# A feed-forward's second matrix product: the plain blocked form against seven block products

## The chip, the core and the metric

One core of a Trainium2 chip. The metric is device time of one execution in microseconds (us), median of the runs. TensorE (PE) multiplies, VectorE (DVE) and ScalarE (ACT) do element-wise work, SyncE (SP) issues nearly all DMA transfers, GpSimd (POOL) has almost nothing to do here. All data are fp32. A difference of under 0.2% is not told from none.

## What is computed

One layer of a hybrid decoder, on 1024 tokens of width 1024. Four mixers come first; the change touches only what follows them:

```python
xn = rmsnorm(h, norm_ffn_w)
gate_up = xn @ w_ffn_in                       # 1024 x 5632
g_ff, u_ff = jnp.split(gate_up, [D_FF], axis=-1)   # D_FF = 2816
h = h + (jax.nn.silu(g_ff) * u_ff) @ w_ffn_out     # 2816 x 1024
return rmsnorm(h, norm_f_w)
```

The last two lines are the *second matrix*: activations (1024 x 2816) times `w_ffn_out` (2816 x 1024), the residual `h` added, and a norm over each row.

## The kernel before

**Precision by three products.** A fp32 operand is split into a high part (an ACT cast to fp32r) and a low part (a DVE subtraction). Each block product is three matmuls: high by high, high by low, low by high. A matmul here takes 128x128 of one operand and 128x512 of the other.

**First matrix.** `ffn_in(j)` makes block j of 22 (128 columns of D_FF, all 1024 tokens): seven block products of 12 matmuls, 84 in all, from operand sums that are already on the chip, with additions from the accumulator banks into SBUF, SiLU on ACT and a multiplication on DVE (lines 1142 to 1144). `prepare(j + 1)` loads and splits the next block's weights (lines 1025 to 1050) in between: its gate half and its up half are two loads on SP. Line 1145 stores a block's result, 128 x 1024, to a DRAM tile `asp[j]`. `j` even uses the four banks `pd`, `j` odd the banks `pq` and `pt`.

**Second matrix.** Two halves of the tokens (`hf`), and in each the 22 blocks j, four tiles of 128 tokens, two halves of the columns, three matmuls (lines 1201 to 1203 in `tile_block`). `load_block(n)` loads a block's weights (line 1156, 512 KB), splits them (1158, 1159), loads the block's activations from `asp` (1166, 256 KB) and splits these (1167, 1168). The last three blocks of a half (`LATE`) are run tile by tile, so that one tile of tokens after the other is finished: line 1224 adds the residual, 1225 squares, `rstd_of` (lines 212 to 222) makes the row's factor by small operations and a square root on ACT, 1230 scales, and 1231 stores the output from ACT's queue.

**Order.** The engines run their own instructions in order. A tile framework has put them in each engine's list in an order of its own, and added the waits. SBUF tiles come from `slot` (128x1024), `half` (128x512) and a ring `tmp` of four 128x512 buffers, `t` in the rows.

Of the kernel before, what the change touches and what calls it, by code (L numbers as in the profile page):

```python
# [38 lines left out]
P = 128  # L39
T = 1024  # L40
D = 1024
# [4 lines left out]
NFF = DFF // P  # L46
EPS = 1e-6
H = 512
# [23 lines left out]
def trunk(ctx: ExitStack, tc: tile.TileContext, x, w_in, w_branch, w_out, w_fin, w_fout, prm_d, gw_d, lw_d,  # L72
          nfw_d, snw_d, cst_d, msk_d, out):
    nc = tc.nc
    V, A, G, TE = nc.vector, nc.scalar, nc.gpsimd, nc.tensor
    mult, add, sub, mx, mn = ALU.mult, ALU.add, ALU.subtract, ALU.max, ALU.min

    cp = ctx.enter_context(tc.tile_pool(name="cp", bufs=1))
    sm = ctx.enter_context(tc.tile_pool(name="sm", bufs=3))
# [21 lines left out]
    slot = Slots("s", 26, (P, T))  # L101
    half = Slots("x", 32, (P, H))
    tmp = ring("t", 4, (P, H))
    wraw = ring("wr", 2, (P, T))
    whi = ring("wh", 2, (P, T), dt=F32R)
    wlo = ring("wl", 2, (P, T), dt=F32R)
    dense_bank = ring("pd", 4, (P, H), pp)
    sbank = ring("pq", 2, (P, H), pp)
    tbank = ring("pt", 2, (P, H), pp)
    bank_at = [0]  # L110

    def allbank():
# [54 lines left out]
    for t in range(NT):  # L167
# [5 lines left out]
        if t % 4 == 3:  # L173
            c = C_LX + t // 4 * P
# [8 lines left out]
    def hs(hf):  # L183
        return slice(hf * H, (hf + 1) * H)
# [23 lines left out]
    def rstd_of(ss, n, inv, table=False):  # L208


        v, r, q = (sm.tile([P, 8], F32, name=a, tag=a)[:, :n] for a in ("v", "r", "q"))
        V.tensor_scalar(v, ss, inv, EPS, op0=mult, op1=add)
        if table:
            A.activation(r, v, AF.Sqrt)
            V.reciprocal(r, r)
        else:
            V.tensor_scalar(r.bitcast(I32), v.bitcast(I32), 1, None, op0=ALU.arith_shift_right)
            V.tensor_scalar(r.bitcast(I32), r.bitcast(I32), -1, 0x5F375A86, op0=mult, op1=add)
        for _ in range(1 if table else 3):
# [235 lines left out]
    for i in range(4):  # L455
        j = A.activation(th[i], th[i], AF.Sqrt, bias=tiny)
# [198 lines left out]
    for i in range(2):  # L655
        w = wv
# [5 lines left out]
    for h in range(4):  # L662
        if h == 3:
# [7 lines left out]
            for t in range(NT):  # L671
                p = dense_bank()
# [29 lines left out]
    for hf in range(2):  # L702
        p = tbank()
# [76 lines left out]
    p = tbank()  # L780
# [22 lines left out]
    for i in range(4):  # L803
        u = sconv(i)
# [144 lines left out]
    dp = ctx.enter_context(tc.tile_pool(name="dp", bufs=1, space=bass.MemoryType.DRAM))  # L949
    hsp = [dp.tile([P, D], F32, name=f"hsp{t}") for t in range(NT)]  # L950
    asp = [dp.tile([P, T], F32, name=f"asp{j}") for j in range(NFF)]

    def two(dt=F32):
        t = slot(dt)
        return t[:, 0:H], t[:, H:T], t
# [139 lines left out]
            slot.free(*wo[0][1])  # L1095


    def ffn_in(j, early=False):
# [12 lines left out]
        y = slot()  # L1111
        u, v, uv = two()
        c21 = tmp()

        def upper():
            product(pa, "A12", "B21", False)
            A.activation(y[:, 0:H], pa, AF.Silu)

        product(pa, "A11", "B11")
        A.copy(u, pa)  # L1120
        yield
        if early:
            upper()
            yield
        product(pd, "S1", "T1")
        yield
        product(pb, "S2", "T2")
        V.tensor_add(u, u, pb)
        yield
        product(pc, "S3", "T3")  # L1130
        V.tensor_add(v, u, pc)
        V.tensor_add(v, v, pd)
        yield
        if not early:
            upper()
# [10 lines left out]
        slot.free(y, uv, *pair.held)  # L1146

    loaded = {}

    def load_block(n):  # L1150

        if n in loaded or n >= 2 * NFF:
            return
        hf, j = n // NFF, n % NFF
        w = wraw()
        nc.sync.dma_start(w, w_fout[j * P:(j + 1) * P, :])
        wh, wl = slot(F32R), slot(F32R)
        A.copy(wh, w)  # L1158
        V.tensor_sub(wl, w, f32(wh))  # L1159
        if n < 2:  # L1160
            h, l, t = two(F32R)
            a = tmp()
        else:
            h, l = half(F32R), half(F32R)
            a = half()
        nc.sync.dma_start(a, asp[j][:, hs(hf)])
        A.copy(h, a)
        V.tensor_sub(l, a, f32(h))
        if n >= 2:
            half.free(a)  # L1170
        loaded[n] = (h, l, wh, wl) if n >= 2 else (h, l, wh, wl, t)

    def drop_block(n):
        b = loaded.pop(n)
        slot.free(*b[2:])
        if n >= 2:
            half.free(b[0], b[1])

    for steps in zip_longest(ffn_in(0, True), ffn_in(1, True)):
# [12 lines left out]
    nfw = slot()  # L1192
    nc.sync.dma_start(nfw, nfw_d.broadcast_to([P, D]))
    LATE = 3

    def tile_block(hf, t, j):
        h, l, wh, wl = loaded[hf * NFF + j][0:4]
        tt = slice(t * P, (t + 1) * P)
        for nh in range(2):
            p = banks[t][nh]  # L1200
            TE.matmul(p, lhsT=h[:, tt], rhs=wh[:, hs(nh)], start=j == 0, stop=False)  # L1201
            TE.matmul(p, lhsT=h[:, tt], rhs=wl[:, hs(nh)], start=False, stop=False)  # L1202
            TE.matmul(p, lhsT=l[:, tt], rhs=wh[:, hs(nh)], start=False, stop=j == NFF - 1)  # L1203

    load_block(1)
    for hf in range(2):
        banks = [[allbank() for nh in range(2)] for t in range(4)]
        for j in range(NFF - LATE):
            load_block(hf * NFF + j + 2)
            for t in range(4):  # L1210
                tile_block(hf, t, j)
            drop_block(hf * NFF + j)
        res = [slot() for t in range(4)]
        for t in range(4):
            nc.sync.dma_start(res[t], hsp[hf * 4 + t])
        for n in range(hf * NFF + NFF - LATE + 2, hf * NFF + NFF + 3):
            load_block(n)
        for t in range(4):
            for j in range(NFF - LATE, NFF):
                tile_block(hf, t, j)  # L1220
            y, sq = slot(), slot()
            ss = sm.tile([P, 8], F32, name="ss", tag="ss")
            for nh in range(2):
                V.tensor_add(res[t][:, hs(nh)], res[t][:, hs(nh)], banks[t][nh])
                A.activation(sq[:, hs(nh)], res[t][:, hs(nh)], AF.Square, accum_out=ss[:, nh:nh + 1])
            V.tensor_add(ss[:, 2:3], ss[:, 0:1], ss[:, 1:2])
            r = rstd_of(ss[:, 2:3], 1, 1.0 / D, True)
            tt = slice((hf * 4 + t) * P, (hf * 4 + t + 1) * P)
            for nh in range(2):
                V.scalar_tensor_tensor(y[:, hs(nh)], res[t][:, hs(nh)], r, nfw[:, hs(nh)], op0=mult, op1=mult)  # L1230
                nc.scalar.dma_start(out[tt, hs(nh)], y[:, hs(nh)])
            slot.free(y, sq)
        for j in range(NFF - LATE, NFF):
            drop_block(hf * NFF + j)
        slot.free(*res)


# ---- launch: one core
# [64 lines left out]
```

## Time and profile before

| | |
|---|---|
| median of 3 runs | 2051.46 us (2050.77 to 2053.79) |
| profiled execution | 2052.34 us |
| its span | 2050.4 us |
| instructions in the span | 23991 |
| PE busy | 2006.1 us (98%), 9892 matmuls |
| DVE busy, ACT busy | 1030.5 us (50%), 632.9 us (31%) |
| mean granted clock of PE | 0.997 |
| chain that ended last | PE 89%, DVE 7%, ACT 2%, issue 1%, DMA 1% |

The span is what the profile sees, from the first instruction to the last; the execution's own time is 1.9 us longer. Busy is the time in which an engine works on an instruction; the chain follows back from the last instruction, at each step, to what released it. A PE that is busy all the time and has the largest share of the chain is the limit over the span as a whole; which wait ends last in a stretch is read from that stretch.

### The profile page before, as it was taken

To read this page: it belongs to the slowest core of one execution; us is meant where nothing else is said; L and a number is where in the kernel's file an instruction comes from. 1 tells how busy PE (TensorE), PEld (TensorE's weight loads), DVE (VectorE), ACT (ScalarE), POOL (GpSimd) and SP (SyncE) were. 2 spreads that over 40 slices of the span, in tenths; PEclk is the share of its full clock that TensorE was granted. 3 is DMA by queue.
4 is the path that set the end of the run, shared out by engine and by line. 5 is a ranking of instruction groups with operands and counts; after the bars stand their busy time and mean duration, and the time that the engine had idled before them with its cause. 6 is when DMAs were issued, how large, how long until landed. Compare 5 with 4: busy or idle time off the path is not lost.

```text
span 2050.4 us, 23991 instructions
## 1 busy us (share of the span) xinstructions
PE 2006.1 (98%) x9892; PEld 1663.1 (81%) x9892; DVE 1030.5 (50%) x1728; ACT 632.9 (31%) x942; POOL 14.2 (1%) x20
## 2 busy tenths in 40 slices
PE   7989999999999999999999999999999999999998
PEld 6779888889888878877779888877888888888886
DVE  6560114765242377566562517268665565554532
ACT  5742112332341111442122323154222232243421
POOL 0000000000000000000000000000000000000000
PEclk9999999999999999999999999999999999999999
DMA  5120111111112110111112014122222222466451
GB/s 172 31 72 11 51 52 32 29 46 42 32 32 61 41 32 21 42 42 31 31 43 66 21 52 154 52 93 83 91 64 93 93 64 91 128 205 221 154 165 41
DMA packets 157772, 147.56 MB, mean 72 GB/s; under 512 B 7472, under 2 KB 134880, under 8 KB 157664
## 3 DMA queue, kind: packets, MB, share of 16 engines
q1 hardware_dynamic: 153824, 136.82, 21.9%
q10 hardware_dynamic: 3840, 9.23, 1.2%
q8 instruction: 77, 1.26, 0.3%
q14 instruction: 31, 0.25, 0.0%
HBM read 126.10 MB, written 19.92 MB: 71 GB/s over the span
## 4 chain that ended last, share of the span: by engine, by line
PE 89%; DVE 7%; ACT 2%; issue 1%; DMA 1%; SPq 0%; DVEq 0%; ACTq 0%
PE pd L199 13%; PE pd L200 13%; PE pd L202 13%; PE pd L1106 3%; PE pd L1105 3%; PE pd L1108 3%; PE pd L318 3%; PE pd L316 3%; PE pd L317 3%; PE pd L1202 2%; PE pd L1203 2%; PE pd L1201 2%; PE pq L1108 2%; PE pq L1106 2%; PE pq L1105 2%; PE pt L1105 1%
## 5 line engine op out<-in xcount | busy, mean ns | idle before, releaser
L199 PE MATMUL pd<-x,wh 128*128 128x512 f32 x1056 | 420.1, 398 | 7.4 <-ACT s L348 7.0
L200 PE MATMUL pd<-x,wh 128*128 128x512 f32 x1056 | 418.1, 396 | 0.0
L152 DVE TENSOR_TENSOR wl<-wr,wh 128x1024 fp32r<-128x1024 f32 x82 | 100.4, 1224 | 370.8 <-PE pd L202 264.4
L202 PE MATMUL pd<-x,wl 128*128 128x512 f32 x1056 | 271.9, 394 | 0.0
L199 PEld LDWEIGHTS pd<-x,wh 128*128 128x128 f32 x1056 | 199.4, 189 | 51.8 <-ACT s L348 7.8
L200 PEld LDWEIGHTS pd<-x,wh 128*128 128x128 f32 x1056 | 199.4, 189 | 41.1 <-issue 2.4
L202 PEld LDWEIGHTS pd<-x,wl 128*128 128x128 f32 x1056 | 196.4, 188 | 42.8 <-issue 3.5
L151 ACT CAST wh<-wr 128x1024 fp32r<-128x1024 f32 x82 | 86.3, 1052 | 249.5 <-PE pd L200 227.8
L316 PE MATMUL pd<-s,x 128*128 128x256 f32 (+2 forms) x512 | 159.5, 312 | 0.6 <-ACT s L151 0.6
L318 PE MATMUL pd<-s,x 128*128 128x256 f32 (+2 forms) x512 | 159.8, 312 | 0.0
L317 PE MATMUL pd<-s,x 128*128 128x256 f32 (+2 forms) x512 | 159.6, 312 | 0.0
L370 ACT ACTIVATE s<-pd 128x512 f32<-128x512 f32 x64 | 38.3, 598 | 217.7 <-PE pd L202 217.7
L316 PEld LDWEIGHTS pd<-s,x 128*128 128x128 f32 x512 | 97.4, 190 | 5.7 <-ACT s L151 0.8
L317 PEld LDWEIGHTS pd<-s,x 128*128 128x128 f32 x512 | 97.5, 190 | 5.1
L318 PEld LDWEIGHTS pd<-s,x 128*128 128x128 f32 x512 | 97.5, 190 | 4.8
L199 PE MATMUL pd<-s,wh 128*128 128x512 f32 x256 | 99.8, 390 | 0.0
L200 PE MATMUL pd<-s,wh 128*128 128x512 f32 x256 | 99.8, 390 | 0.0
L382 DVE SCALAR_TENSOR_TENSOR s<-s,pd 128x512 f32<-128x512 f32 x64 | 43.9, 687 | 94.5 <-PE pd L202 94.5
L1159 DVE TENSOR_TENSOR s<-wr,s 128x1024 fp32r<-128x1024 f32 x44 | 53.9, 1225 | 69.0 <-ACT s L1158 54.2
L523 DVE COPY_PREDICATED s<-msk,pq 128x256 f32<-128x256 uint8 x128 | 61.9, 555 | 29.6 <-PE pq L517 16.2
L1025 ACT CAST wh<-wr 128x1024 fp32r<-128x1024 f32 x22 | 23.2, 1055 | 161.7 <-PE pq L1106 79.6
L202 PE MATMUL pd<-s,wl 128*128 128x512 f32 x256 | 68.5, 389 | 0.0
(341 smaller groups left out, 3560.4 us busy)
## 6 DMA issues: line engine op xcount, KB each, us to landing
wr<-in_w_in SPq DMA_DIRECT2D x76, 512.0 KB, 3.6
wr<-in_w_fin SPq DMA_DIRECT2D x44, 512.0 KB, 4.6
wr<-in_w_fout SPq DMA_DIRECT2D x44, 512.0 KB, 3.6
asp<-s SPq DMA_DIRECT2D x22, 512.0 KB, 4.9
x<-asp SPq DMA_DIRECT2D x42, 256.0 KB, 3.9
wr<-in_w_branch SPq DMA_DIRECT2D x16, 512.0 KB, 3.3
s<-in_x SPq DMA_DIRECT2D x8, 512.0 KB, 7.4
wr<-in_w_out SPq DMA_DIRECT2D x8, 512.0 KB, 3.9
```

What stands on the lines that cost most here:

```text
L151: i = A.copy(h, raw)
L152: V.tensor_sub(l, raw, f32(h))
L199: TE.matmul(p, lhsT=wh[k], rhs=ah, start=k == 0, stop=False)
L200: TE.matmul(p, lhsT=wh[k], rhs=al, start=False, stop=False)
L202: TE.matmul(p, lhsT=wl[k], rhs=ah, start=False, stop=k == n - 1)
L316: TE.matmul(p, lhsT=ah, rhs=wh, start=k == 0, stop=False)
L317: TE.matmul(p, lhsT=ah, rhs=wl, start=False, stop=False)
L318: TE.matmul(p, lhsT=al, rhs=wh, start=False, stop=k == n - 1)
L523: V.copy_predicated(dst[:, :, :, side, :], m, pv_[ab][:, i].rearrange("p c (n h) -> p c n h", h=h))
L1105: TE.matmul(p, lhsT=ah[:, k], rhs=bh, start=first and k == 0, stop=False, skip_group_check=True)
L1106: TE.matmul(p, lhsT=ah[:, k], rhs=bl, start=False, stop=False, skip_group_check=True)
L1108: TE.matmul(p, lhsT=al[:, k], rhs=bh, start=False, stop=k == KH - 1, skip_group_check=True)
```

## The change

The second matrix is computed by seven block products (Winograd's form of Strassen's method). The activations are cut into 2 x 2 quarters by tokens (first and second 512) and by even and odd blocks of D_FF; the weights by even and odd blocks and by column halves. Each product has 11 steps (one per pair of blocks), and a step is four tiles of 128 tokens by three matmuls. The products are taken in the order 1, 5, 6, 2, 7, 3, 4 of `steps`.

- **Left sums.** `row_sums(k)`, at the end of each odd `ffn_in`, makes four sums or differences of the pair's activation quarters (lines 1106, 1107, 1108 and, in the next block, 1113) and stores each, 256 KB, to a DRAM tile `ssp[k][i]` (lines 1110, 1114) on SP.
- **Right sums.** `split_step` makes the sums of the weights in place, one DVE subtraction in each step of products 5, 6, 7 and 4 (line 1214).
- **Loads.** `load_step` loads a quarter block of weights, 256 KB, in each step of products 1, 5, 6 and 2 (line 1186) and a quarter block of activations or sums in every step (line 1203), into the `tmp` ring. Loads stand seven steps ahead and splits (1224, 1225) four.
- **ffn_in.** Two intermediate tiles come from the `tmp` ring; the last block takes its product of A12 and B21 early, and steps 0 to 2 are loaded during that block.
- **Ends.** `after(n, t)` adds a product's banks into the result tiles (1291 to 1311); `finish` (1279 to 1285) norms and stores a row tile. Rows 0 to 3 are finished after product 3, at the start of product 4, rows 4 to 7 at the end.

```diff
+    def row_sums(k):
+        y0, y1 = ys_of.pop(2 * k), ys_of.pop(2 * k + 1)
+        a11, a21, a12, a22 = y0[:, 0:H], y0[:, H:T], y1[:, 0:H], y1[:, H:T]
+        s1 = tmp()
+        V.tensor_add(s1, a21, a22)
+        V.tensor_sub(a21, a11, a21)
+        V.tensor_sub(a11, s1, a11)
+        for i, t in enumerate((s1, a11, a21)):
+            nc.sync.dma_start(ssp[k][i], t)
+        def last():
+            V.tensor_sub(a12, a12, a11)
+            nc.sync.dma_start(ssp[k][3], a12)
+            slot.free(y0, y1)
+        later.append(last)
...
-        u, v, uv = two()
+        if own:
+            u, v, uv = two()
+        else:
+            u, v = tmp(), tmp()
...
         A.copy(u, pa)
+        while later:
+            later.pop()()
...
         nc.sync.dma_start(asp[j], y)
+        if j % 2:
+            row_sums(j // 2)
...
+    steps = [(n, k) for n in (1, 5, 6, 2, 7, 3, 4) for k in range(KO)]
+    def load_step(i):
+        n, k = steps[i]
+        if n == 1:
+            we[k] = slot()
+            load_rows(2 * k, 0, we[k])
+        elif n == 5:
+            load_rows(2 * k, 1, we[k])
+        elif n == 6:
+            wd[k] = slot()
+            load_rows(2 * k + 1, 1, wd[k])
+        elif n == 2:
+            load_rows(2 * k + 1, 0, wd[k])
+        a = araw[i] = tmp()
+        nc.sync.dma_start(a, {1: asp[2 * k][:, 0:H], 2: asp[2 * k + 1][:, 0:H], 3: ssp[k][3], 4: asp[2 * k + 1][:, H:T],
+                              5: ssp[k][0], 6: ssp[k][1], 7: ssp[k][2]}[n])
+    def split_step(i, own=False):
+        if n in (5, 6, 7, 4):
+            dst, x, y = {5: (b11, b12, b11), 6: (b11, b22, b11), 7: (b12, b22, b12), 4: (b11, b21, b11)}[n]
+            V.tensor_sub(dst, x, y)
...
+        for h, l, x in ((bh, bl, b), (ah, al, a)):
+            A.copy(h, x)
+            V.tensor_sub(l, x, f32(h))
+    def step_mm(i, t, p):
+        TE.matmul(p, lhsT=ah[:, tt], rhs=bh, start=new, stop=False, skip_group_check=True)
+        TE.matmul(p, lhsT=ah[:, tt], rhs=bl, start=False, stop=False, skip_group_check=True)
+        TE.matmul(p, lhsT=al[:, tt], rhs=bh, start=False, stop=end, skip_group_check=True)
...
         if j == NFF - 1:
-            load_block(0)
-        for steps in ffn_in(j):
+            for i in range(3):
+                load_step(i)
+            for i in range(2):
+                split_step(i, True)
+        for _ in ffn_in(j, j == NFF - 1):
             pass
...
+    def finish(t, row):
+        for nh in range(2):
+            A.activation(sq, row[nh], AF.Square, accum_out=ss[:, nh:nh + 1])
+        V.tensor_add(ss[:, 2:3], ss[:, 0:1], ss[:, 1:2])
+        r = rstd_of(ss[:, 2:3], 1, 1.0 / D, True)
+        for nh in range(2):
+            V.scalar_tensor_tensor(row[nh], row[nh], r, nfw[:, hs(nh)], op0=mult, op1=mult)
+            nc.scalar.dma_start(out[t * P:(t + 1) * P, hs(nh)], row[nh])
...
+    for i in range(3, 7):
+        load_step(i)
+    for i in range(2, 4):
+        split_step(i)
+    for i, (n, k) in enumerate(steps):
+        load_step(i + 7)
+        split_step(i + 4)
+        if n == 4 and k >= KO - LATE:
+            continue
+        for t in range(4):
+            step_mm(i, t, (down if n in (5, 2, 3) else up)[t])
+        drop_step(i)
+        if k == KO - 1:
+            for t in range(4):
+                after(n, t)
+    lastr = [res(4 + t, 0) for t in range(4)]
+    for t in range(4):
+        for i in range(len(steps) - LATE, len(steps)):
+            step_mm(i, t, up[t])
+        after(4, t)
```

SP in the first matrix, before: what it issues from block 14's store to block 16's (`wr<-in_w_fin` are weights of the first matrix, gate and up half in turn).

```order
L1145 DMA asp14_9111<-s_11723 128x1024
L145 DMA wr_11950<-in_w_fin 128x8x128
L145 DMA wr_12075<-in_w_fin 128x8x128
L1145 DMA asp15_9112<-s_11850 128x1024
L145 DMA wr_12077<-in_w_fin 128x8x128
L145 DMA wr_12202<-in_w_fin 128x8x128
L1145 DMA asp16_9113<-s_11977 128x1024
```

The same place of the change (`ssp7_0` to `ssp7_3` are the four left sums of blocks 14 and 15).

```order
L1171 DMA asp14_9111<-s_11840 128x1024
L145 DMA wr_12078<-in_w_fin 128x8x128
L145 DMA wr_12206<-in_w_fin 128x8x128
L1171 DMA asp15_9112<-s_11970 128x1024
L1110 DMA ssp7_0_9147<-t_12069 128x512
L1110 DMA ssp7_2_9149<-s_11840 128x512
L1110 DMA ssp7_1_9148<-s_11840 128x512
L145 DMA wr_12208<-in_w_fin 128x8x128
L1114 DMA ssp7_3_9150<-s_11970 128x512
L145 DMA wr_12341<-in_w_fin 128x8x128
L1171 DMA asp16_9113<-s_12105 128x1024
```

Behind each odd block's store stand now three more stores, each waiting for a DVE sum, ahead of the next load of the up half.

SP at the hand-over to the second matrix, in the change (`t<-asp` are the activations of steps 3 and on; those of steps 0 to 2 stand further ahead).

```order
L1171 DMA asp21_9118<-s_12764 128x1024
L1110 DMA ssp10_0_9159<-t_12863 128x512
L1110 DMA ssp10_1_9160<-s_12635 128x512
L1110 DMA ssp10_2_9161<-s_12635 128x512
L1203 DMA t_12890<-asp6_9103 128x512
L1114 DMA ssp10_3_9162<-s_12764 128x512
L1203 DMA t_12894<-asp8_9105 128x512
L1203 DMA t_12898<-asp10_9107 128x512
L1203 DMA t_12902<-asp12_9109 128x512
```

The loads of steps 3 to 6 stand behind the last block's store and the last left sums' stores. Before, the loads of the second matrix stood ahead of the last block's store (`asp1` to `asp7`) or right behind it.

DVE at the end of the change, from the last addition of a product's bank on (`pd_12877` is row 7's bank, line 1284 the scaling).

```order
L1311 TENSOR_TENSOR x_14762<-x_14762,pd_12877 128x512
L212 TENSOR_SCALAR v_14835<-ss_14830 128x1
...
L222 SCALAR_TENSOR_TENSOR r_14836<-q_14837,r_14836 128x1
L1284 SCALAR_TENSOR_TENSOR x_14758<-x_14758,r_14808,s_12872 128x512
L1284 SCALAR_TENSOR_TENSOR wh_12884<-wh_12884,r_14808,s_12872 128x512
L1284 SCALAR_TENSOR_TENSOR x_14760<-x_14760,r_14836,s_12872 128x512
L1284 SCALAR_TENSOR_TENSOR wh_12885<-wh_12885,r_14836,s_12872 128x512
L1281 TENSOR_TENSOR ss_14858<-ss_14858 128x1
L212 TENSOR_SCALAR v_14863<-ss_14858 128x1
```

The scalings of rows 5 and 6 stand between row 7's addition and the small operations for row 7. Before, one row's two scalings were done ahead of the last row's chain.

## Rows read from the trace of the kernel before

**Rows 1.** The page, part 1: engine, busy us, share of span, instructions.

```profile
PE 2006.1 (98%) x9892; PEld 1663.1 (81%) x9892; DVE 1030.5 (50%) x1728; ACT 632.9 (31%) x942; POOL 14.2 (1%) x20
```

**Rows 2.** Table by stretch: length, each engine's busy us, granted clock, DMA share, GB/s.

```profile
1583.26:1602.30 19.04, 19.04 (x85) 15.77 (x84) 11.33 (x15) 5.28 (x7) 0.00 (x0) 1.00 0.26 83
1802.00:1821.04 19.04, 19.04 (x85) 15.77 (x84) 10.87 (x12) 7.43 (x10) 0.00 (x0) 1.00 0.72 236
1500.00:1600.00 100.00, 100.00 (x443) 82.81 (x442) 58.76 (x78) 28.06 (x38) 0.00 (x0) 1.00 0.29 91
```

**Rows 3.** PE's waits, 1300 us to the end, the two largest of five groups: us, times, longest.

```profile
PE pd L1106 <- DVE s L970: 2.0, 4, 0.7
PE pd L1105 <- ACT s L969: 1.7, 4, 0.5
```

**Rows 4.** PE timeline at both ends of the second matrix: start, duration, instruction.

```profile
1802.23 0.39 PE L1201 MATMUL pt<-s 128*128 128x512 f32 x1
...
2041.37 0.39 PE L1203 MATMUL pd<-s,x 128*128 128x512 f32 x1
```

**Rows 5.** Timeline of the tail.

```profile
2041.79 0.69 DVE L1224 TENSOR_TENSOR s<-s,pd 128x512 f32<-128x512 f32 x1
...
2045.24 0.16 DVE L220 TENSOR_TENSOR q<-r 128x1 f32<-128x1 f32 x1
...
2045.83 1.41 DVE L1230 SCALAR_TENSOR_TENSOR s<-s,r 128x512 f32<-128x512 f32 x2
2046.61 1.00 ACTq L1231 DMA_DIRECT2D out<-s  x2
```

**Rows 6.** Timeline over an odd block's end and the block behind it.

```profile
1575.76 0.69 DVE L1144 TENSOR_TENSOR s<-s 128x512 f32<-128x512 f32 x1
...
1577.98 0.68 DVE L1050 TENSOR_TENSOR s<-wr,s 128x512 fp32r<-128x512 f32 x1
...
1578.69 16.45 SPq L145 DMA_DIRECT2D wr<-in_w_fin  x2
...
1582.18 0.69 DVE L1128 TENSOR_TENSOR s<-s,pd 128x512 f32<-128x512 f32 x1 [3.52 <-PE pd L1108]
...
1586.16 0.68 DVE L1034 TENSOR_TENSOR s<-wr 128x512 f32<-128x512 f32 x1
...
1591.67 1.22 DVE L1042 TENSOR_TENSOR s<-s 128x1024 fp32r<-128x1024 f32 x1
...
1595.52 0.39 PE L1105 MATMUL pt<-x,s 128*128 128x512 f32 x1
```

**Rows 7.** DMA, 1555 to 1605 us: GB/s in 40 slices; issues, median us to landing.

```profile
GB/s 0 0 110 234 404 345 162 10 0 0 0 0 0 0 13 0 0 70 229 401 333 212 13 0 0 0 0 0 0 0 0 0 43 208 367 360 261 31 7 0
...
wr<-in_w_fin SPq DMA_DIRECT2D x6, 512.0 KB, 4.8
asp<-s SPq DMA_DIRECT2D x3, 512.0 KB, 5.0
```

**Rows 8.** Line 1166, the activation loads: landing.

```profile
DMA to landing us min/median/max: 2.5/3.9/6.7
```

**Rows 9.** Groups by shape, 1760 us to the end: busy us, mean ns, idle before.

```profile
L1167 ACT CAST x<-x 128x512 fp32r<-128x512 f32 x42 | 25.9, 617 | 38.7 <-DMA x<-asp 31.5 <-PE pd L1202 7.0
```

**Rows 10.** PE timeline behind two earlier waits of PE.

```profile
106.27 0.50 PE L199 MATMUL pd<-x,wh 128*128 128x512 f32 x1 [1.71 <-ACT s L348]
...
122.71 0.80 PE L199 MATMUL pd<-x,wh 128*128 128x512 f32 x1 [5.26 <-ACT s L348]
123.30 0.63 PE L200 MATMUL pd<-x,wh 128*128 128x512 f32 x1
123.73 0.63 PE L199 MATMUL pd<-x,wh 128*128 128x512 f32 x1
```

**Rows 11.** Table by stretch, behind these two waits.

```profile
122.70:127.00 4.30, 4.29 (x10) 3.42 (x11) 3.19 (x5) 2.48 (x4) 0.00 (x0) 0.50 0.00 0
106.20:110.00 3.80, 3.73 (x16) 3.11 (x17) 3.80 (x4) 3.75 (x5) 0.00 (x0) 1.00 0.48 138
```

More of the change, by code (lines that the diff above doesn't have):

```diff
@@ L951, in trunk @@
     asp = [dp.tile([P, T], F32, name=f"asp{j}") for j in range(NFF)]
+    ssp = [[dp.tile([P, H], F32, name=f"ssp{k}_{i}") for i in range(4)] for k in range(NFF // 2)]
     def two(dt=F32):
@@ L1095, in trunk, with ffn_in @@
             slot.free(*wo[0][1])
-    def ffn_in(j, early=False):
+    ys_of, later = {}, []
+    def row_sums(k):
[12 more added lines that the diff above has]
+        later.append(last)
+    def ffn_in(j, early=False, own=False):
         pair = pairs.pop(j)
@@ L1110, in ffn_in @@
         pa, pb, pc, pd = (sbank(), tbank(), sbank(), tbank()) if j % 2 else (dense_bank() for i in range(4))
-        y = slot()
-        u, v, uv = two()
+        y = ys_of[j] = slot()
+        if own:
+            u, v, uv = two()
+        else:
+            u, v = tmp(), tmp()
         c21 = tmp()
@@ L1145, in ffn_in @@
         nc.sync.dma_start(asp[j], y)
[L1146 to L1152, printed above, removed]
-            return
[L1154 to L1162, printed above, removed]
-        else:
[L1164 to L1179, printed above, removed]
+        slot.free(*pair.held)
+        if own:
+            slot.free(uv)
+        if j % 2:
+            row_sums(j // 2)
+    KO = NFF // 2
+    LATE = 3
+    steps = [(n, k) for n in (1, 5, 6, 2, 7, 3, 4) for k in range(KO)]
+    we, wd, araw, parts_of, taken = {}, {}, {}, {}, {}
+    def load_rows(j, c, to):
+        nc.sync.dma_start(to[:, hs(c)], w_fout[j * P:(j + 1) * P, hs(c)])
@@ new lines, in load_step @@
+    def load_step(i):
+        if i >= len(steps):
+            return
+        n, k = steps[i]
[12 more added lines that the diff above has]
+                              5: ssp[k][0], 6: ssp[k][1], 7: ssp[k][2]}[n])
@@ new lines, in split_step @@
+    def split_step(i, own=False):
+        if i >= len(steps):
+            return
+        n, k = steps[i]
+        b11, b12 = we[k][:, 0:H], we[k][:, H:T]
+        b21, b22 = (wd[k][:, 0:H], wd[k][:, H:T]) if k in wd else (None, None)
+        if n in (5, 6, 7, 4):
+            dst, x, y = {5: (b11, b12, b11), 6: (b11, b22, b11), 7: (b12, b22, b12), 4: (b11, b21, b11)}[n]
+            V.tensor_sub(dst, x, y)
+        b = {1: b11, 2: b21, 3: b22, 4: b11, 5: b11, 6: b11, 7: b12}[n]
+        if own:
+            (ah, al, t0), (bh, bl, t1) = two(F32R), two(F32R)
+            taken[i] = slot, (t0, t1)
+        else:
+            ah, al, bh, bl = (half(F32R) for _ in range(4))
+            taken[i] = half, (ah, al, bh, bl)
+        a = araw.pop(i)
+        for h, l, x in ((bh, bl, b), (ah, al, a)):
+            A.copy(h, x)
+            V.tensor_sub(l, x, f32(h))
+        parts_of[i] = ah, al, bh, bl
@@ new lines, in step_mm, with drop_step @@
+    def step_mm(i, t, p):
+        n, k = steps[i]
+        ah, al, bh, bl = parts_of[i]
+        tt = slice(t * P, (t + 1) * P)
+        new, end = n in (1, 5, 2, 3) and k == 0, k == KO - 1
+        TE.matmul(p, lhsT=ah[:, tt], rhs=bh, start=new, stop=False, skip_group_check=True)
+        TE.matmul(p, lhsT=ah[:, tt], rhs=bl, start=False, stop=False, skip_group_check=True)
+        TE.matmul(p, lhsT=al[:, tt], rhs=bh, start=False, stop=end, skip_group_check=True)
+    def drop_step(i):
+        pool, ts = taken.pop(i)
+        pool.free(*ts)
+        parts_of.pop(i)
@@ L1180, in trunk @@
+    for _ in zip_longest(ffn_in(0, True, True), ffn_in(1, True, True)):
         pass
@@ L1185, in trunk @@
         if j == NFF - 1:
-            load_block(0)
-        for steps in ffn_in(j):
-            pass
+            for i in range(3):
[3 more added lines that the diff above has]
+        for _ in ffn_in(j, j == NFF - 1):
+            pass
+    while later:
+        later.pop()()
     half.free(*op_halves)
@@ L1193, in trunk @@
     nc.sync.dma_start(nfw, nfw_d.broadcast_to([P, D]))
[L1194 to L1198, printed above, removed]
-        for nh in range(2):
[L1200 to L1209, printed above, removed]
-            for t in range(4):
[L1211 to L1235, printed above, removed]
@@ new lines, in four, with res @@
+    def four(take):
+        a, b = take(F32), take(F32)
+        return a[:, 0:H], a[:, H:T], b[:, 0:H], b[:, H:T]
+    up, down = [dense_bank() for t in range(4)], [(sbank, tbank)[t % 2]() for t in range(4)]
+    c11, c22, c12 = four(wraw), four(whi), four(wlo)
+    def res(t, nh):
+        r = half()
+        nc.sync.dma_start(r, hsp[t][:, hs(nh)])
+        return r
+    def finish(t, row):
+        ss = sm.tile([P, 8], F32, name="ss", tag="ss")
+        sq = half()
+        for nh in range(2):
+            A.activation(sq, row[nh], AF.Square, accum_out=ss[:, nh:nh + 1])
+        half.free(sq)
+        V.tensor_add(ss[:, 2:3], ss[:, 0:1], ss[:, 1:2])
[3 more added lines that the diff above has]
+            nc.scalar.dma_start(out[t * P:(t + 1) * P, hs(nh)], row[nh])
@@ new lines, in after @@
+    def after(n, t):
+        if n == 1:
+            r = res(t, 0)
+            V.tensor_add(c11[t], r, up[t])
+            half.free(r)
+        elif n == 5:
+            A.copy(c22[t], down[t])
+        elif n == 6:
+            r = res(t, 1)
+            V.tensor_add(c12[t], c22[t], up[t])
+            V.tensor_add(c12[t], c12[t], r)
+            half.free(r)
+        elif n == 2:
+            V.tensor_add(c11[t], c11[t], down[t])
+        elif n == 7:
+            r = res(4 + t, 1)
+            V.tensor_add(c22[t], c22[t], up[t])
+            V.tensor_add(c22[t], c22[t], r)
+            half.free(r)
+        elif n == 3:
+            V.tensor_add(c12[t], c12[t], down[t])
+            finish(t, (c11[t], c12[t]))
+        else:
+            V.tensor_add(lastr[t], lastr[t], up[t])
+            finish(4 + t, (lastr[t], c22[t]))
```

## Prediction

> **What bounds the kernel now.** First the busy table [rows 1]: TensorE (PE) is busy 98% of the span, VectorE (DVE) 50%, ScalarE (ACT) 31%. The reader is to see which engine has no room, and that DVE and ACT have half. Second, because shares are averages, the table of stretches [rows 2]: in the first matrix 443 matmuls start in 100 us, one per 0.2257 us, with the clock at 1.00, while DVE and ACT are busy 59 and 28 of 100; in the second matrix it is 10.9 and 7.4 of 19.04. Third, PE's waits from 1300 us on [rows 3]: five groups, 5 us together, the largest 2.0; all wait for operands of the feed-forward's beginning, and none lies in the second matrix. Fourth, the PE timeline at both ends of the second matrix [rows 4]: it runs from 1802.23 to 2041.37, and 1055 start-to-start steps in 239.14 us are 0.2267 us each. So PE alone sets the time, and a matmul that goes is worth 0.2267 us as long as the new helper work keeps PE fed. Last, the tail [rows 5]: from the last matmul's start, L = 2041.37 [rows 4], to the span's end at 2050.4 are 9.03 us, and there DVE sets the pace.
>
> **What it removes.** Plain: 2 x 22 x 4 x 2 x 3 = 1056 matmuls. Seven products: 7 x 11 x 4 x 3 = 924 of the same shape. 132 fewer x 0.2267 = **-29.9 us**.
>
> **What it adds, part by part.**
>
> *Left sums beside the first matrix.* Per pair of column blocks: four DVE operations of 128x512 (0.69 each [rows 6]) and four stores of 256 KB. A block's period is 84 matmuls, 19.04 us, DVE busy 11.33 of it [rows 2], so a pair has 38.08 with 22.7 used and gets 2.8 more: hidden. The stores go through SP, and there something is queued behind them: the next load of the up half of the first matrix. Before, SP issued it at 1578.69, when line 1050 (of before) had freed its buffer [rows 6]. Now it stands behind the store that waits for the third sum (line 1108 of the change), some 4.4 us behind the start of the product of line 1144 (of before) (three 0.69 operations, and the split operations of 1.2 and 0.7 between them): 1580.5, 1.9 us later. Landing took 4.8 us [rows 7], so it is there at 1585.4 instead of 1583.5, and DVE's first use is at 1586.16 [rows 6]. The chain from that use to PE has more room: the split of the sums S1 and S2 ends at 1592.9 and their first product starts at 1595.52 [rows 6], 2.6 us. The stores move 1 MB more in a stretch that moves about 1.5 MB; if all of it were ahead of the load, at the 400 GB/s peak of [rows 7], it would cost 2.5 us. Even then (1587.9, 1.7 late) the room of 2.6 suffices. The fourth sum waits for the store of the block to DRAM to land (5.0 us [rows 7]: about 1581.5, and the next DVE work of that block comes at 1582.18): at most some tenths, not on PE's path. I take **0**; ends 0 and, if loads landed 3 us later still, 10 transitions x 2 = 20 (a rival, below).
>
> *Hand-over from the last block to the first product.* Call the last first-matrix matmul's start E (1802.00 before, one matmul ahead of the 1802.23 of [rows 4]). PE has 33 matmuls for after E, the rest of steps 0 to 2, so step 3 is due at E + 7.5. Its activation load stands on SP behind the last block's store and three stores of sums. By DVE's order the last product is made at about E + 2, the three sums follow by E + 5 and one of their stores waits for each: the load is issued at about E + 5.4. A load of this kind took 2.5, 3.9 and 6.7 us (least, median, most [rows 8]); with 3.5 and a cast of 0.62 [rows 9] step 3 starts at E + 9.6: a wait of 2.2 us (1.2 to 5.4 with those ends). The loads of steps 4 to 6 stand behind the fourth store, which waits for the last block's store to land: 0.2 us more. With it an earlier load (step 1's), whose cast stands on ACT ahead of the copy that PE's next product needs, 0.3 at the median landing (0 to 2.5), and 0.1 for a DVE row that the steps' splits delay. Together **+2.8** (1.3 to 8).
>
> *Steady steps.* A step is 12 matmuls, 2.72 us. DVE has two splits and at most one right sum, 3 x 0.69 = 2.07; ACT two casts, 1.24. Loads: 512 KB or less per step, at most 193 GB/s, against the 236 GB/s that the DMA engines moved at a share of 0.72 [rows 2]. The four buffers for loaded activations turn over in about 0.4 + 3.9 + 0.62 + 0.69 = 5.6 us, so one is free every 1.4. The parts are made four steps, 10.9 us, ahead, so that the eight eviction operations at the end of a product (5.5 us of DVE) are hidden. I take **0**; ends 0 and, if landing stayed at the 6.7 maximum, still 0 (8.4 / 4 = 2.1 < 2.72).
>
> *Start of the seventh product.* Rows 0 to 3 are finished there: four times two squares on ACT, a chain of small operations, two scalings of 0.75 on DVE, and output stores that ACT issues, 0.5 each [rows 5], all ahead of the splits of step 70. The splits of steps 66 to 69 are done by then. The fourth row's work ends about 11.9 us behind the product's first start, step 70 is due at 11.5: **+0.5** (0 to 2).
>
> *Tail.* Before, a row of output had 18 matmuls between its end and the next row's (4.08 us), and about 3.3 us of DVE. Now a row has half its columns left, 9 matmuls, 2.04 us, and still needs two squares, the chain and two scalings. So the last four rows pile up on DVE, and by the order rows 5 and 6 scale four times ahead of the last row's chain. Followed with the gaps of [rows 5] (0.19 per small operation, 0.66 per scaling, 0.5 per issued store), the last scaling ends at L + 9.2 instead of L + 5.87 (2047.24): **+3.3** (2 to 4.5).
>
> **Sum:** -29.9 + 2.8 + 0.5 + 3.3 = -23.3. The profiled execution took 2052.34 (span 2050.4), so it would take 2029.0; the median of the three is 0.9 below it, and the forecast for the median is **2028.2 us**.
>
> **A rule beside a row.** In this trace PE once waited 5.26 us, and the matmuls behind it started 0.43 us apart (twelve of them) with a granted clock of 0.50, the 1.2 GHz level; behind a wait of 1.71 us the clock stayed at 1.00 [rows 10, 11]. Such a drop costs 12 x (0.43 - 0.2267) = 2.4 us. My waits at the hand-over, 2.2 and less, are nearer to the second, so I add nothing; should one reach some 5 us, it is 2030.6. The Trainium skill, "TensorE: Matmul & The Clock Gate", section "What's actually happening", says that an idle array falls to half its rate and comes back only after sustained work; taken by itself it would have the clock fall at the hand-over and speaks against a change that brings waits to an engine that had none. The 1.71 us row is against taking it so broadly.
>
> **Rivals.**
> 1. *The gain is kept nearly whole*: the hand-over loads land in 2.5 us as the quickest did, the tail overlaps better. -29.9 + 1.2 + 2 = -26.7, 2025. For it: landings of 2.5 us are seen [rows 8]. Against: SP's order holds the load back whatever the landing. Chance 0.25.
> 2. *Each odd-to-even transition stalls PE*: loads behind the stores land late, 10 x 0.5 to 1.5. Adds 5 to 15: 2033 to 2043. For it: SP is one queue and DMA's peak is reached there [rows 7]. Against: the 2.6 us of room. Chance 0.17.
> 3. *The clock falls at the hand-over*, because the wait there is longer than I have it, with loads that take 6 us: 2.4, or 2.4 and 2.5 more, 2030.6 to 2033. For it: the wait of 5.26 us [rows 10]. Against: the one of 1.71. Chance 0.13.
> 4. *Slower than before: the steps starve.* If each of the 77 steps took longer than PE's 2.72 us, the new bound would be the round of the four activation buffers. All gain is gone when a step takes 2.72 + 23.3/77 = 3.02 us, a round of 12.1, a landing of 10.4 us; at 12 us of landing (13.7 round, 3.43 a step) it costs 55, 2083. For it: every step now waits for an activation load of its own, and only four are in flight. Against: no such load took more than 6.7 us [rows 8], in a stretch where more was moved. Chance 0.03.
> 5. *The change does not do what it says*, e.g. the left sums' operations end up on PE's path: between 2043 and 2056, around no change. Chance 0.04.
>
> **How the numbers follow.** My case (2026.5 to 2031) 0.38, rivals 0.25, 0.17, 0.13, 0.03, 0.04. The range from 2023 to 2040 holds nearly all of mine, rivals 1 and 3, and most of 2; what is left out is about 0.15. A measurement of this kernel tells some 0.2%, 4 us, from no change: faster 0.93, same 0.03, slower 0.04.
>
> **What would show it.** Right: 9760 matmuls; the seven products 0.2267 us per matmul without waits; one PE wait of about 2 us on a cast some 7 us behind the last first-matrix matmul; no PE wait in the blocks before it; from the last matmul's start to the end about 12.3 us instead of 9.0. Wrong: PE waits at each odd block's end (rival 2), PE waits on ACT or DVE throughout the products with those waiting on loads (rival 4), a granted clock under 1 behind the hand-over (rival 3).

## The result

| | before | changed |
|---|---|---|
| median | 2051.65 us (2050.77 to 2053.79, 4 runs) | 2028.12 us (2027.17 to 2029.08, 4 runs) |
| ratio, 95% interval | | 0.9884 (0.9867 to 0.9901) |
| profiled execution, its span | 2052.34, 2050.4 us | 2027.17, 2025.4 us |
| matmuls | 9892 | 9760 |
| last matmul's start to the span's end | 9.0 us | 10.8 us |

The change is 23.5 us faster, within 0.1 us of the forecast. The question for the rest is whether it is so for the reasons given. Some of its terms were mis-sized, and one that it left out is there.

The page of the changed kernel, its span and part 1, beside [rows 1]:

```profile
span 2025.4 us, 24187 instructions
...
PE 1977.7 (98%) x9760; PEld 1639.5 (81%) x9760; DVE 1107.2 (55%) x1898; ACT 651.4 (32%) x1012; POOL 14.2 (1%) x20
```

PE is as full as before, with 132 matmuls fewer. DVE has 77 us more work, ACT 19 us more.

PE's waits from 1300 us on, against [rows 3] (lines of the changed kernel):

```profile
PE pd L1127 <- DVE s L971: 2.0, 4, 0.7
PE pd L1233 <- ACT x L1224: 1.9, 1, 1.9
PE pd L1126 <- ACT s L970: 1.7, 4, 0.5
```

The waits of lines 1126 and 1127 are those of before. The new one is of 1.9 us, at line 1233, the steps' first matmul, on a cast (line 1224): this is the hand-over. There is none at the odd blocks' ends, none in the later steps, none at the start of the seventh product. The table by stretch says what the products look like:

```profile
1802.00:1811.00 9.00, 7.82 (x35) 6.15 (x33) 4.75 (x7) 0.63 (x1) 0.00 (x0) 1.00 0.98 360
...
1812.70:1816.40 3.70, 3.70 (x11) 2.91 (x11) 2.70 (x5) 2.39 (x5) 0.00 (x0) 0.57 0.89 293
...
1820.00:1900.00 80.00, 80.00 (x354) 66.28 (x354) 68.73 (x114) 39.29 (x71) 0.00 (x0) 1.00 0.62 201
1900.00:2000.00 100.00, 100.00 (x442) 82.84 (x442) 60.23 (x117) 44.02 (x87) 0.00 (x0) 1.00 0.39 120
```

From 1820 to 2000, 796 matmuls start in 180 us, 0.226 us each as before [rows 2], with DVE at 86 and 60% and DMA at 0.62 and 0.39. That is the steady stretch as forecast. The first two lines are not: DMA is at 0.98 over the hand-over, and behind it the granted clock is 0.57 over 3.7 us, most of them at the lower level, 1.2 GHz. The PE timeline there:

```profile
1809.43 0.39 PE L1235 MATMUL pd<-x 128*128 128x512 f32 x1
1811.70 0.50 PE L1233 MATMUL pd<-x 128*128 128x512 f32 x1 [1.88 <-ACT x L1224]
...
1812.75 0.68 PE L1235 MATMUL pd<-x 128*128 128x512 f32 x2
1813.22 0.63 PE L1233 MATMUL pd<-x 128*128 128x512 f32 x1
1813.65 0.63 PE L1234 MATMUL pd<-x 128*128 128x512 f32 x1
...
1816.21 0.58 PE L1234 MATMUL pd<-x 128*128 128x512 f32 x1
...
1817.09 0.39 PE L1234 MATMUL pd<-x 128*128 128x512 f32 x1
```

PE is idle for 1.88 us. From one matmul's start to the next it is 2.27 us (1809.43 to 1811.70) in place of 0.23, so step 3 starts 2.0 us late. The next matmuls start 0.34 and then 0.24 us apart, about the old pace; from 1813.22 on, 1.5 us behind the wait, they are 0.43 us apart until 1816.6. From 1811.70 to 1817.09 are 16 steps: 5.39 us in place of 3.63, 1.76 us lost. Why the load is late is seen on SP, and its cast on ACT (a row that gathers several issues gives the time from the first to the end of the last):

```profile
1804.71 0.33 SPq L1171 DMA_DIRECT2D asp<-s  x1
1805.44 0.33 SPq L1110 DMA_DIRECT2D ssp<-t  x1
1806.89 0.80 SPq L1110 DMA_DIRECT2D ssp<-s  x2
1807.79 0.41 SPq L1203 DMA_DIRECT2D t<-asp  x1
...
1811.03 0.62 ACT L1224 CAST x<-t 128x512 fp32r<-128x512 f32 x1 [7.07 <-DMA t<-asp]
```

Step 3's load goes out at 1807.79, behind the block's store and the three sums' stores. The last first-matrix matmul starts at 1802.18 (E), so this is E + 5.6, forecast E + 5.4. It is cast at 1811.03, 3.2 us later, and PE starts at 1811.70, E + 9.5, forecast E + 9.6.

The odd block's end, in the order of [rows 6] (load of the up half, its first use on DVE, split of the sums, first product of these):

```profile
1579.51 0.39 SPq L145 DMA_DIRECT2D wr<-in_w_fin  x1
...
1585.12 0.69 DVE L1035 TENSOR_TENSOR s<-wr 128x512 f32<-128x512 f32 x1
...
1590.63 1.22 DVE L1043 TENSOR_TENSOR s<-s 128x1024 fp32r<-128x1024 f32 x1
...
1594.47 0.39 PE L1126 MATMUL pt<-x,s 128*128 128x512 f32 x1
```

The load goes out 4.8 us behind the product of the block (line 1170, at 1574.71) instead of 2.9, 1.9 us later as forecast; it is used at the same distance as before, and the split ends 2.6 us ahead of its product, as before.

The tail, in place of [rows 5]:

```profile
2014.52 0.39 PE L1235 MATMUL pd<-x 128*128 128x512 f32 x1
...
2016.32 0.28 DVE L220 TENSOR_TENSOR q<-r 128x1 f32<-128x1 f32 x2
...
2018.89 0.75 DVE L1284 SCALAR_TENSOR_TENSOR wh<-wh,r,s 128x512 f32<-128x512 f32 x1
...
2020.06 0.20 ACT L214 ACTIVATE r<-v 128x1 f32<-128x1 f32 x1 [2.48 <-DVE v L212]
...
2021.74 0.75 DVE L1284 SCALAR_TENSOR_TENSOR wh<-wh,r,s 128x512 f32<-128x512 f32 x1
...
2022.52 0.34 ACTq L1285 DMA_DIRECT2D out<-wh  x1
```

The last scaling ends at 2022.49, L + 8.0 (L = 2014.52): 2.1 us later than before's L + 5.9, forecast 3.3. The pile-up is there: rows 5 and 6 scale until 2019.6, and only then can row 7's chain begin, though its bank was added at 2015.22. ACT issues a store in 0.34 us. So it did before: the 1.00 us of the row of two stores in [rows 5] runs from the first issue to the end of the second, with the wait for the second scaling in it, and is not twice 0.5.

**The account of the spans:** 132 x 0.2267 = -29.9; wait +2.0; slow matmuls +1.8; tail +1.8; together -24.3. The spans differ by 25.0. The rest is ahead of E: in this execution the first matmul of the feed-forward starts at 1371.6 instead of 1372.6 us, and the stretch from there to E took 0.3 more, once four matmuls of step 0 that now stand in it are taken off.

### The profile page after: what moved, and what is told of

The parts are those of the page before. It is cut to its first block, busy times and chain, and to the rows that moved or that the text cites. A ratio compares the mean times of both kernels' runs of the same rounds, so it can differ in the third digit from the quotient of the medians.

```text
span 2025.4 us, 24187 instructions
## 1 busy us (share of the span) xinstructions
PE 1977.7 (98%) x9760; PEld 1639.5 (81%) x9760; DVE 1107.2 (55%) x1898; ACT 651.4 (32%) x1012; POOL 14.2 (1%) x20
## 4 chain that ended last, share of the span: by engine, by line
PE 88%; DVE 7%; ACT 2%; DMA 1%; issue 1%; SPq 0%; DVEq 0%; ACTq 0%
PE pd L199 13%; PE pd L202 13%; PE pd L200 13%; PE pd L1127 3%; PE pd L1129 3%; PE pd L1126 3%; PE pd L318 3%; PE pd L316 3%; PE pd L317 3%; PE pd L1233 2%; PE pq L1127 2%; PE pq L1129 2%; PE pd L1235 2%; PE pq L1126 2%; PE pd L1234 2%; PE pq L517 1%
## 5 line engine op out<-in xcount | busy, mean ns | idle before, releaser
L152 DVE TENSOR_TENSOR wl<-wr,wh 128x1024 fp32r<-128x1024 f32 x82 | 100.4, 1224 | 371.5 <-PE pd L202 264.3
L1225 DVE TENSOR_TENSOR x<-s,x 128x512 fp32r<-128x512 f32 x75 | 51.7, 689 | 40.2 <-ACT x L1224 40.2
```

The lines of the kernel that those rows point to most:

```text
L152: V.tensor_sub(l, raw, f32(h))
```

## Experiments

Each is made from the changed kernel; its line numbers shift by a few. E is the start of the last first-matrix matmul and L of the last matmul in each execution. *Queue theory* is the prediction's account of the hand-over: the load of step 3 is late because of its place on SP. Its rival, *landing theory*: it is late because DMA is full there, wherever the load stands. Runs of one kernel lie up to 3 us apart (2027.06 to 2029.97 in experiment 6), so differences of 1 or 2 us are read from stretches of the trace and not from medians or single runs.

**1. The loads ahead of the last stores** (`held_back` holds the last block's store and its three sums' stores; the fourth sum follows them).

```diff
...
-        nc.sync.dma_start(asp[j], y)
...
+        if j == NFF - 1:
+            held_back.append(store)
+        else:
+            store()
...
-    for i in range(3, 7):
+    for i in range(3, 6):
         load_step(i)
+    for f in held_back:
+        f()
+    while later:
+        later.pop()()
+    load_step(6)
```

> On SP the activation loads of steps 3 to 5 stand ahead of the last block's store and the last left sums' stores. Queue theory: the load of step 3 is issued some 3.5 us earlier, right behind the SiLU that frees its buffer, PE's wait of 1.9 us at the hand-over is gone, and with it the stretch at the lower clock behind it (1.8 us): 3.6 us less than the changed kernel, about 2024.5. Landing theory (the load is late because DMA is at 360 GB/s there, wherever it stands on SP): a wait of 1.5 us or more stays, and the time stays within 1 us of the changed kernel's 2028.1.

Measured: 2024.20 us (2023.75 to 2025.16, 4 runs), ratio to before 0.9869 (0.9852 to 0.9885); 3.9 us under the changed kernel. SP at the hand-over, and the cast of step 3:

```profile
1802.43 3.47 SPq L1215 DMA_DIRECT2D t<-asp  x3
1805.95 0.42 SPq L1178 DMA_DIRECT2D asp<-s  x1
...
1807.72 0.62 ACT L1236 CAST x<-t 128x512 fp32r<-128x512 f32 x1 [2.90 <-DMA t<-asp]
```

And all of PE's waits from 1400 us on, one at the feed-forward's beginning:

```profile
PE pd L1133 <- DVE s L971: 0.7, 1, 0.7
```

Step 3's load goes out at E - 0.6 (1802.43; E = 1803.05), 6.2 us earlier than in the changed kernel and not 3.5; those of steps 4 and 5 follow. It lands later, 5.3 us behind its issue instead of 3.2, so that the cast at E + 4.7 is 4.2 us earlier. PE does not wait, though DMA moves 398 GB/s over 1802.9 to 1811.9, more than the 360 of the changed kernel. The clock is at 1.00 to the last matmul. So the place on SP decides whether PE waits, and the landing takes back a part of what an earlier issue gives. From E to L (2011.58) it is 208.5 us for 920 steps, 0.2267 each, instead of 212.3: the 3.8 us are the wait and the slow stretch together, so the slow stretch was the wait's doing.

**2. Only one store behind the load** (the third sum's store, which waits for line 1108).

```diff
+            if k == NFF // 2 - 1 and i == 1:
+                held_back.append((ssp[k][i], t))
+            else:
+                nc.sync.dma_start(ssp[k][i], t)
...
+    load_step(3)
+    for o, t in held_back:
+        nc.sync.dma_start(o, t)
...
```

> Only the store that waits for the third left sum is moved behind step 3's load. Queue theory: the load is issued about 1.2 us earlier, and PE's wait falls from 1.9 to about 0.7 us. For the clock: if it follows the wait, a wait of 0.7 leaves it at 1.00 behind the hand-over (no matmuls 0.43 us apart); if the slow stretch comes from something else there, it stays. Landing theory: the wait stays above 1.5.

Measured: 2028.42 us (one run). A miss for the queue theory as I had put it. Step 3's load and its cast, and PE behind the hand-over:

```profile
1808.36 0.41 SPq L1206 DMA_DIRECT2D t<-asp  x1
...
1812.11 0.62 ACT L1227 CAST x<-t 128x512 fp32r<-128x512 f32 x1 [6.95 <-DMA t<-asp]
...
1812.78 0.50 PE L1236 MATMUL pd<-x 128*128 128x512 f32 x1 [1.75 <-ACT x L1227]
...
1817.03 0.50 PE L1236 MATMUL pd<-x 128*128 128x512 f32 x1 [1.23 <-ACT x L1227]
```

The wait is 1.75 us, not 0.7, and a second one of 1.23 follows at step 4. Step 3's load went out at E + 5.0 (1808.36; E = 1803.39), only 0.6 earlier than in the changed kernel, and took 3.75 us to its cast instead of 3.24, which came at E + 8.7, 0.1 earlier. Here the small step forward was eaten by the landing, so the landing theory has a part. Step 4's load stands behind the fourth sum's store as in the changed kernel and was issued at E + 7.3, as there (E + 7.4), but was cast at E + 13.0 instead of E + 11.8: this is landing alone. For the clock: behind 1.75 us of wait the matmuls stayed 0.23 us apart, with a granted clock of 1.00.

**3. Three more stores ahead of the load** (and the fourth sum's store with them).

```diff
             nc.sync.dma_start(ssp[k][i], t)
+            if k == NFF // 2 - 1:
+                nc.sync.dma_start(spare[i], t)
```

> Each of the last three left sums is stored once more, to DRAM that nobody reads, and step 3's load comes to stand behind the fourth sum's store too. Queue theory: the load is issued about 1.7 us later, PE waits 3.5 us instead of 1.9, and the clock falls behind the wait as before, some 1.8 to 2.4 us of slow matmuls: about 2 us longer than the changed kernel. Landing theory: the wait stays within 0.5 us of 1.9.

Measured: 2031.01 us (one run), 2.9 above the changed kernel. Step 3's load, and PE behind its wait:

```profile
1810.38 2.14 SPq L1206 DMA_DIRECT2D t<-asp  x4
...
1814.94 0.79 PE L1236 MATMUL pd<-x 128*128 128x512 f32 x1 [4.71 <-ACT x L1227]
1815.53 0.63 PE L1237 MATMUL pd<-x 128*128 128x512 f32 x1
...
1819.25 0.40 PE L1237 MATMUL pd<-x 128*128 128x512 f32 x1
```

The wait is 4.7 us, more than the 3.5 expected: the load goes out at E + 7.8 (E = 1802.59) and is cast 3.9 us later. A later place on SP makes a longer wait, as the queue theory has it. Behind the wait the clock is at the lower level at once, and the matmuls are 0.43 us apart. From 1814.94 to 1819.25 are ten steps, 2.0 us lost.

**4. The last six steps row by row.**

```diff
-    LATE = 3
+    LATE = 6
```

> The last six steps instead of three are run tile by tile, so that the last rows end 18 matmuls (4.1 us) apart as in the kernel before, not 9 (2.0 us). Pile-up theory: rows wait for each other on DVE at the end only because 2.0 us is less than a row's DVE work; the time from the last matmul's start to the end of the span falls from 10.9 to about the 9.0 of before, 1.9 us less in all, about 2026.2. Rival (the longer end is the last row's own chain, its in-place scaling and its stores): it stays at 10.9 and the time at 2028.1.

Measured: 2026.86 us (2026.20 to 2027.25, 4 runs), ratio 0.9881 (0.9866 to 0.9895); 1.3 us under the changed kernel, whose runs these overlap; so the tail is read from the trace:

```profile
2016.09 0.39 PE L1235 MATMUL pd<-x 128*128 128x512 f32 x1
...
2021.83 0.74 DVE L1284 SCALAR_TENSOR_TENSOR wh<-wh,r,s 128x512 f32<-128x512 f32 x1
```

L = 2016.09, the last scaling ends at L + 6.5 instead of L + 8.0, and the span at 2025.4, 9.35 us behind L instead of 10.83. The pile-up theory holds, for 1.5 of the 1.8 us. The span of this execution is no shorter than the changed kernel's (2025.4 too), since its E is 0.9 us later, and its hand-over, with a wait of 2.2, costs 0.7 more.

**5. Both edits, 1 and 4.**

```diff
-    LATE = 3
+    LATE = 6
...
-    for i in range(3, 7):
+    for i in range(3, 6):
         load_step(i)
+    for f in held_back:
+        f()
...
```

> The two edits together: step 3 to 5's loads ahead of the last stores on SP, and the last six steps run tile by tile. If the hand-over (1.9 us of wait and 1.8 us of slow matmuls) and the tail are separate costs, their gains add: 2024.2 - 1.4 = about 2022.8, no PE wait behind 1400 us but those at the feed-forward's beginning, and 9.3 us from the last matmul's start to the end. If one gives the other back, it stays at 2024.

Measured: 2022.14 us (2021.23 to 2023.01, 4 runs), ratio 0.9859 (0.9843 to 0.9876). The two gains add: 5.2 us from the medians above, 6.0 here. In the trace, E (1802.30) to L (2010.84) is 208.5 us, as in experiment 1, and L to the span's end 9.35, as in experiment 4: 5.3 us less together. This is the fastest kernel here.

**6. No left sums** (for the first ten pairs; their products read the plain activations, so the output is another and only the time counts).

```diff
+        if k < NFF // 2 - 1:
+            slot.free(y0, y1)
+            return
         s1 = tmp()
...
+        s = ssp[k] if k == KO - 1 else [asp[2 * k + c // 2][:, hs(c % 2)] for c in range(4)]
...
```

> The left sums of the first ten pairs are neither made nor stored, and the products read the plain activations in their place, so the result is another one and only the time counts. Theory (the sums lie wholly beside the first matrix): the time stays within 1 us of the changed kernel's 2028.1, and PE has no more and no fewer waits. Rival (they cost something at each odd block's end): 5 us or more are gained.

Measured: 2028.18 us (2027.06 to 2029.97, 4 runs), ratio 0.9889 (0.9874 to 0.9904), against 2028.12. The 40 DVE operations and 40 stores (10 MB) cost nothing that these runs can tell.

**7. Three of these four stores twice** (for the first ten pairs).

```diff
             nc.sync.dma_start(ssp[k][i], t)
+            if k < NFF // 2 - 1:
+                nc.sync.dma_start(spare[k][i], t)
```

> Each of the three left sums of the first ten pairs is stored once more, to DRAM that nobody reads, ahead of the load of the up half on SP: that load goes about 1.2 us later and 0.75 MB more move at the same time (1.9 us at 400 GB/s). Theory (2.6 us of room, of which the change used nothing that PE sees): waits of PE at the ten transitions of 0 to 0.5 us each, at most 5 us in all. Rival (the room was already gone): 1 us or more at each, 10 us or more.

Measured: 2027.06 us (one run); PE waits nowhere in the blocks behind the feed-forward's beginning, before the hand-over. The same places of the timeline as for the changed kernel:

```profile
1582.01 11.70 SPq L145 DMA_DIRECT2D wr<-in_w_fin  x2
...
1587.45 0.68 DVE L1036 TENSOR_TENSOR s<-wr 128x512 f32<-128x512 f32 x1
...
1590.24 1.22 DVE L1044 TENSOR_TENSOR s<-s 128x1024 fp32r<-128x1024 f32 x1
...
1594.08 0.39 PE L1129 MATMUL pt<-x,s 128*128 128x512 f32 x1
```

The load goes out at 1582.01, 2.9 us later than in the changed kernel once the 0.4 is allowed for by which this execution is ahead, and its first use is at 1587.45, 2.7 later. But the split of the sums starts at the same distance from its product, 3.8 us ahead. The room was larger than I had it. In this kernel's DVE order another split (line 1028) stands ahead of that use, and the idle times of 0.9 and 0.7 us that DVE has behind it in the changed kernel are gone.

**8. Two more DVE operations in each step with a right sum** (products 5, 6, 7 and 4). In three of these products `z` is the tile that is written, so that the sums come out as zero; the time counts.

```diff
             V.tensor_sub(dst, x, y)
+            z = x if n == 5 else y
+            V.tensor_add(dst, dst, z)
+            V.tensor_sub(dst, dst, z)
```

> Two more DVE operations of 128x512 in each step of products 5, 6, 7 and 4 (a tile added and taken away again), so that DVE has five where it had three: 3.05 us at 0.61 from start to start, against 2.72 of PE. Theory (a step is free as long as DVE stays under 2.72 us): DVE becomes the bound in these 44 steps, 44 x 0.33 = 15 us longer, 8 to 30 with the lead of four steps and the gaps behind waits. Rival (DVE is not near its limit, or the round of the activation buffers is the limit and not DVE): within 2 us of 2028.1.

Measured: 2027.64 us (one run): nothing lost in the steps, a miss. PE's one wait behind the feed-forward's beginning is at the hand-over (2.9 us, 1.0 more than in the changed kernel). The table by stretch (PE, weight loads, DVE, ACT busy), this kernel's and then the changed kernel's:

```profile
1910.00:1940.00 30.00, 30.00 (x134) 24.83 (x133) 30.00 (x51) 14.48 (x26) 0.00 (x0) 1.00 0.38 112
...
1910.00:1940.00 30.00, 30.00 (x134) 24.84 (x133) 16.68 (x28) 12.57 (x22) 0.00 (x0) 1.00 0.34 97
```

DVE is full from 1910 to 1940, where the changed kernel's is busy 16.68 us, and PE does not see it. My sum took a step by itself, 0.33 us by 44, as if a sum were made in the step that uses it. The sums of line 1214 in the two kernels (first and last start) show another picture:

```profile
L1214 DVE TENSOR_TENSOR s<-s x44: 683/690/694, 1781.4 to 1876.9; 128x512 f32<-128x512 f32 x44
...
L1214 DVE TENSOR_TENSOR s<-s x44: 678/681/692, 1781.0 to 1974.2; 128x512 f32<-128x512 f32 x44
```

In the changed kernel all 44 sums are begun by 1876.9, though the seventh product, which uses the last eleven, starts at 1984.8: DVE's order has them far more than four steps ahead. So what counts is DVE's idle time over the whole run. From 1820 to 2000 it was busy 129.0 of 180 us in the changed kernel and is 173.6 here: the added work went into the gaps and nearly filled them, and the last sum still came ahead of its product.

**9. Four more.**

```diff
             V.tensor_sub(dst, x, y)
+            for _ in range(2):
+                V.tensor_add(dst, dst, x)
+                V.tensor_sub(dst, dst, x)
```

> Four more DVE operations in each step of products 5, 6, 7 and 4, seven in all: 7 x 0.61 = 4.3 us a step against 2.72 of PE. Theory (a lead of four steps, 10.9 us, hides DVE's backlog, and products without right sums, where DVE needs 1.2 of 2.72 us, give it back): products 5 and 6 lose 22 x 1.55 - 10.9 = 23 us, the two products 7 and 4 each 11 x 1.55 - 10.9 = 6: some 35 us more, about 2063, slower than the kernel before, with PE's waits on DVE in these products alone. Rival (DVE has still room, as with five): within 5 us of 2028.

Measured: 2068.59 us (one run), 40 above the changed kernel and above the kernel before. PE's waits from 1400 us on:

```profile
PE pd L1236 <- ACT x L1227: 17.2, 13, 6.0
PE pq L1237 <- DVE x L1228: 5.8, 3, 2.1
```

24 us of waits with the hand-over's 2, nearly all in the steps. DVE has hardly a gap left, and none in this stretch:

```profile
1940.00:1980.00 40.00, 36.83 (x154) 27.98 (x153) 40.00 (x68) 13.42 (x24) 0.00 (x0) 1.00 0.28 81
```

The granted clock is 0.97, 0.94 and 0.89 from 1845 to 1905, 1980 to 2010 and 2010 to 2055. From start to start, E to L takes 250.9 us instead of 212.3, 38.6 more, and the tail 13.5 instead of 10.8: together 41.3 of the 41.4 us by which the spans differ. So the slower side of the forecast exists, with DVE as the bound: five operations a step fit into DVE's time here, seven do not. The change itself has three.

## Why the prediction was right, step by step

- **-29.9 for 132 matmuls:** right. 0.226 us per matmul with DVE at up to 86% (table by stretch), PE never waits in the steady steps, and without the wait at the hand-over the whole second matrix runs at 0.2267 (experiment 1).
- **Left sums, 0:** right, shown by experiments 6 and 7. The late load was 1.9 us later as worked out (its 4.4 us behind the product and its time of 1580.5 do not fit each other; 4.7 is what the time says, and 4.8 was measured). The room behind it was understated.
- **Hand-over, +2.8 of waiting:** the mechanism was right, shown by experiments 1 and 3; step 3 was 2.0 us late where I had 2.2, and the 0.6 of smaller terms did not show. That the load's landing changes with its place on SP (3.2 us in the changed kernel, 5.3, 3.75 and 3.9 in experiments 1, 2 and 3) was not in the sum.
- **"My waits at the hand-over are nearer to the second, so I add nothing" (the clock):** this failed. The clock did fall behind 1.88 us of wait, for 1.8 us, and with it came the prediction's own sign of being wrong, a granted clock under 1 behind the hand-over. Two rows, of 1.71 and 5.26 us, could not say what a wait of 2 us does; the runs have 1.75 without a fall, and 1.88 and 2.2 with one. Rival 3 held the mechanism, with too long a wait as its condition and 2.4 as its price. The rule of the Trainium skill ("TensorE: Matmul & The Clock Gate", section "What's actually happening") ties the lower rate to idleness and does not say that a wait as short as this one is enough. So the prediction took it too broadly when it had the rule call the fall; the runs are what shows it.
- **Start of the seventh product, +0.5:** it was 0. Step 70 was due four steps, 10.9 us, behind the product's first start (the prediction has 11.5), and started then, at 1995.71, without a wait. The fourth row's scalings, 1994.95 to 1996.37, did not stand ahead of its splits as I had it but behind them; the last of these ended at 1995.03.
- **Tail, +3.3:** the mechanism was right, shown by experiment 4, the size too large: 1.8, with 10.8 us from L to the end where I had 12.3. The last scaling ended at L + 8.0 where I had 9.2. Small operations of two rows overlap (two in 0.28 us at 2016.32), and the 0.5 us per issued store was misread from the row of two: it is 0.34. How the 1.2 us divide between these is not shown.

So 2.8 + 0.5 + 3.3 = 6.6 forecast, 2.0 + 1.8 + 1.8 = 5.6 measured in one span; the clock's 1.8 that I left out stood against 2.8 too much in three other terms. That the medians agree to 0.1 us is luck (the two profiled executions differ by 25.0, the medians by 23.5); that the gain is some 24 and not 30 is not.

## What to carry to other kernels

When a product is saved, price the ends: between two stages the first loads of the new stage belong ahead of the last stores of the old one on the issuing queue (3.8 us here), and rows that finish faster than their own finishing work pile up at the end (1.5 us here). Side work that can be done well ahead of its use is free until the engine's idle time over the whole run is used up (from 1820 to 2000 DVE was busy 129.0, then 173.6 of 180 us without loss), so sum it over the run and not per step. A wait of PE of about 2 us can cost as much again behind it, in matmuls at the lower clock (2.0 and 1.8 us here).

## What was not expected of the hardware

The clock can fall at the same place in one execution and not in another. At the beginning of the feed-forward, where PE has short waits that the change does not touch, the stretch from 1388 to 1400 us has the full clock in the changed kernel's profile, by the table by stretch:

```profile
1388.00:1400.00 12.00, 8.30 (x29) 4.49 (x28) 11.48 (x19) 6.49 (x12) 0.00 (x0) 1.00 0.18 53
```

The same stretch of the kernel of experiment 5 has not:

```profile
1388.00:1400.00 12.00, 10.21 (x26) 6.37 (x27) 11.48 (x19) 6.63 (x12) 0.00 (x0) 0.72 0.21 63
```

26 matmuls start there instead of 29. From the feed-forward's first matmul to its last in the first matrix it is 430.6 us in the changed kernel, and 431.3, 431.5 and 431.2 in experiments 3, 2 and 5, which had the fall. So some 0.6 to 0.9 us of the difference between executions come from it. Six of the eleven profiled executions had a fall there (in experiment 7 a shorter one that cost nothing). What decides it in an execution is not settled here.

Behind E the runs show more than the two cases of 1.75 and 1.88 us. Ten waits there were of 1.88 us or more (in the changed kernel and in experiments 3, 4, 6, 7, 8 and, four times, 9), and with each the clock was at the lower level soon behind the wait or already in it. The waits of 1.75 us and less, in experiments 2 and 9, had none. The beginning of the feed-forward, with waits of at most 0.7 us close together, shows that this is no rule for the length of one wait alone.
